# Feed-forward of a hybrid block: up products by seven products of halves, up and down in separate pieces

## The chip, the cores and the metric

The kernel runs on one core of a Trainium2 chip. The metric is the device time of one execution in microseconds: the median of three runs was 3004.93 us before the change (3002.14 to 3009.09). One further execution was profiled, and it gives the trace. The core has four engines for arithmetic that work side by side, each through its own queue in order: TensorE (PE in the rows; PEld is its weight load), VectorE (DVE), ScalarE (ACT) and GpSimd (POOL). SyncE (SP) issues all DMA transfers of this kernel, in order too.

## The reference

One layer over 2048 tokens of 1024 channels: a mixer of three kinds of heads (gated delta rule, mLSTM, S5), an output projection with a residual, and a gated feed-forward with a short causal convolution, again with a residual, and a last norm. The change touches the feed-forward alone:

```
def conv_ffn(x, w_up, conv_w, conv_b, w_down):
    h = causal_depthwise_conv(x @ w_up, conv_w) + conv_b      # 1024 -> 5632, three taps
    gate, up = jnp.split(h, 2, axis=-1)
    return (jax.nn.silu(gate) * up) @ w_down                  # 2816 -> 1024
```

Everything is float32. With 2048 tokens the up product has 2048 x 1024 x 5632 multiplications and the down product half of that.

## The kernel before, in words

A float32 product is made of three faster ones. Each operand is split into a high part (rounded to the format fp32r, by an ACT copy) and a low part (the difference, by a subtraction on POOL or DVE), and `mm` issues for each pair of tiles high x high, high x low and low x high into one PSUM bank.

Work is written as Python generators. `drive` steps them: it keeps a clock of estimated costs, takes the first generator whose needs are met at PE's estimated time, sides before the main one, and lets it emit its next instructions. All engines' calls go through one helper, so that every row of the profile names its line, 167, and the tiles tell the rows apart. The order on each engine is fixed when the program is built. Within one generator the instructions stand in the order of its text, and on the chip each engine takes its queue in that order, waiting at an instruction until what it needs is there.

**Mixer and output projection** (to about 1536 us). `out_proj` runs over 16 tiles of 128 tokens. When the mixer's heads are done, `ffn_pools` opens the pools of the feed-forward, and each tile that is projected is also normed, transposed (`norm2`) and, for the first 1024 tokens, split into the two resident tiles `h2h` and `h2l`; the other 1024 tokens go to memory (`h2_d`). After the last tile `up_first` issues the first four up products.

**Feed-forward** (`ffn`). Tokens come in two halves of 1024, middle channels in 22 tiles of 128; up tile i makes the gate and up tile 22 + i the factor. `jobs` lists, for each half, two up jobs and then a down job over a group of two middle tiles. An up job does, for both sides and both blocks of 512 tokens, one product of 24 matmuls (8 tiles of 128 input channels x 3) into a bank, then the convolution (two small copies of the halo, ACT copy and ACT Identity out of PSUM, two scalar-tensor-tensor on DVE), and for each block Silu, the product and its split into `f_mh` and `f_ml`, which stay in SBUF. A down job does, for 8 tiles of 128 tokens x 2 halves of the output, 6 matmuls into a bank and then adds the bank to `f_acc` in SBUF (DVE), where x plus the output projection already is. Weights are loaded and split (ACT, POOL) by `Weights`, 1024 columns at a time, some tiles ahead. After the last group of a half `final_sums` and `finals` do the last norm and store.

Of the kernel before, what the change touches and what calls it, by code (L numbers as in the profile page):

```python
# [35 lines left out]
Q_BUFS, Z_BUFS = 4, 4  # L36
C_ID, C_TRI, C_CAPT, C_CAPD, C_MASK, C_UP = 0, 1, 2, 3, 4, 5
# [3 lines left out]
def f32(ap):  # L41
    return ap.bitcast(F32)
# [144 lines left out]
class Hybrid:  # L187
# [55 lines left out]
    def params(self):  # L243
# [46 lines left out]
        self.h2_d = self.dram.tile([KD, P, HALF], F32, name="h2_d")  # L290
# [1171 lines left out]
    def part(self, kind):  # L1462
        return self.fw.tile([P, KD, P], F32R, tag=kind, bufs=4, name=kind)

    def raw(self):
        return self.fw.tile([P, KD, P], F32, tag="f_wr", bufs=2, name="f_wr")

# [3 lines left out]
    def ffn_pools(self):  # L1471

        self.wctx.close()
        self.lctx.close()
        self.pctx.close()
        self.ps = self.pool("ps2", space=PSUM)
        self.bufs = {"big": 5, "sd": 3, "y": 1, "yh": 2, "yl": 2}
        kp = self.pool("kp", ctx=self.rctx)
        self.h2t = [kp.tile([P, KD, HALF], F32R, name=f"h2{e}") for e in "hl"]
        self.h2 = [[t[:, k, :] for k in range(KD)] for t in self.h2t]  # L1480
        self.fw = self.pool("fw", ctx=self.rctx)
        self.op = self.pool("op", ctx=self.octx)
        self.ffn_plan()

    def out_proj(self):
# [60 lines left out]
        for i in range(n):  # L1546
# [4 lines left out]
            if i >= n - 2:  # L1551
                self.fws.load()
            if i == n - 1:
                self.fws.split()
# [4 lines left out]
        yield lambda: all(i in self.normed for i in range(HALF // P))  # L1559
        yield from self.up_first()  # L1560

    def norm2(self, i, x, r):

        self.A.activation(out=x, in_=x, func=AF.Copy, scale=r)
        t0 = i * P % HALF
        for j in range(0, KD, 4):
# [15 lines left out]
    class Weights:  # L1582

        def __init__(self, k, order):
            self.k, self.order, self.n = k, order, 0
            self.rawq, self.rdy = [], []

        def load(self):
            if self.n >= len(self.order) or len(self.rawq) >= 2:
                return  # L1590
            kind, m = self.order[self.n]
            self.n += 1
            t, k = self.k.raw(), self.k
            if kind == "u":
                k.S.dma_start(out=t, in_=k.ins["w_up"][0][:, m * P:(m + 1) * P].rearrange("(k p) c -> p k c", p=P))
            else:
                k.S.dma_start(out=t.rearrange("p k c -> p (k c)"), in_=k.ins["w_down"][0][m * P:(m + 1) * P, :])
            self.rawq.append(t)

        def split(self):  # L1600
            if not self.rawq:
                return
            w = self.rawq.pop(0)
            hi, lo = self.k.part("f_wh"), self.k.part("f_wl")
            self.k.split(hi, lo, w)
            self.rdy.append((hi, lo))
            self.load()

        def ahead(self, n):
            if len(self.rdy) < n:  # L1610
                self.split()

        def take(self, n):
            while len(self.rdy) < n:
                self.split()
            r, self.rdy = self.rdy[:n], self.rdy[n:]
            return r

    def ffn_plan(self):
        self.groups = [[m, m + 1] for m in range(0, MF, 2)]  # L1620
        NH = L // HALF

        self.jobs = jobs = []
        for hf in range(NH):
            for gi, g in enumerate(self.groups):
                for j, m in enumerate(g):
                    jobs.append(("U", hf, m))
                    if j == (gi == len(self.groups) - 1) and gi:
                        jobs.append(("D", hf, gi - 1))
            jobs.append(("D", hf, len(self.groups) - 1))  # L1630
        order = []
        for kind, hf, i in jobs:
            order += [("u", i), ("u", MF + i)] if kind == "U" else [("d", m) for m in self.groups[i]]
        self.fws = self.Weights(self, order)

    def up_prod(self, wh, wl, q):
        hh, hl = self.h2
        yield wl, "big"
        ps = self.ps.tile([P, BT], F32, tag="big", bufs=5, name="psf")
        qq = slice(q * BT, (q + 1) * BT)  # L1640
        yield from self.mm3(ps, [(wh[:, k, :], wl[:, k, :], hh[k][:, qq], hl[k][:, qq]) for k in range(KD)])
        return ps

    def up_first(self):
        self.u0 = []
        for side in range(2):
            (wh, wl), = self.fws.take(1)
            for q in range(2):
                self.u0.append((yield from self.up_prod(wh, wl, q)))
                self.fws.ahead(2)  # L1650

    def ffn(self, fp):
        V, A, G, T, S, ins = self.V, self.A, self.G, self.T, self.S, self.ins
# [292 lines left out]
```

## Time and profile before

| | us |
|---|---|
| median of 3 runs | 3004.93 |
| the profiled execution | 3009.54 |
| its span, first to last instruction | 3007.8 |
| PE busy | 2791.7 (93%) |
| DVE busy | 1945.4 (65%) |
| ACT busy | 1165.5 (39%) |
| POOL busy | 821.1 (27%) |
| first up product starts at | 1536.15 |
| last down matmul starts at | 2987.16 |
| mean granted PE clock | 0.965 |

A row of grouped instructions reads: line, engine, operation, output<-inputs by the names of tiles, partitions x elements and types, x count | busy us in all, mean ns of one | idle us of the engine just before them, and who ended it. A row of the timeline reads: start us, length us, engine, line, operation, with the idle time before it in brackets. Matmuls are pipelined, so that a matmul's own duration (389 ns) is longer than the distance to the next one.

### The profile page before, as it was taken

How to read it: one execution, taken by the hardware profiler on the slowest of the kernel's cores; microseconds unless marked ns; L12 is line 12 of the kernel's file. 1: busy time of each engine (PE TensorE's matmuls, PEld its weight loads, DVE VectorE, ACT ScalarE, POOL GpSimd, SP SyncE). 2: the span in 40 equal slices, each digit the busy share in tenths (PEclk: the TensorE clock that was granted, in tenths of full speed). 3: DMA queues.
4: the chain of work that ended last, by engine and by line, in shares of the span. 5: the costliest groups of instructions: out<-in, count | busy, mean ns of one | idle time of the engine just before them, and what ended most of it. 6: DMA issues, size and time to landing. Idle time of an engine off the chain costs nothing.

```text
span 3007.8 us, 37696 instructions
## 1 busy us (share of the span) xinstructions
PE 2791.7 (93%) x13826; PEld 2327.6 (77%) x13826; DVE 1945.4 (65%) x4400; ACT 1165.5 (39%) x2202; POOL 821.1 (27%) x536
## 2 busy tenths in 40 slices
PE   7797789988998989889999999999999999999997
PEld 5686677877886878578888888888888888888885
DVE  6875667678765886664455656566567655656566
ACT  4444344444544354633333332233344323333333
POOL 3261122223322243123222222222222222222223
PEclk9898889989999999989999999999999999999998
DMA  4233212233222324334561111111134111111111
GB/s 121 63 96 94 76 47 77 56 84 103 62 58 68 85 78 123 99 94 141 167 204 42 49 49 50 42 50 56 43 101 165 49 43 49 51 48 50 50 44 62
DMA packets 314944, 232.39 MB, mean 77 GB/s; under 512 B 36291, under 2 KB 286278, under 8 KB 314758
## 3 DMA queue, kind: packets, MB, share of 16 engines
q1 hardware_dynamic: 314758, 229.98, 26.0%
q8 instruction: 109, 1.79, 0.3%
q14 instruction: 77, 0.63, 0.1%
HBM read 192.06 MB, written 37.88 MB: 76 GB/s over the span
## 4 chain that ended last, share of the span: by engine, by line
PE 56%; DVE 3%; ACT 1%; issue 0%; DMA 0%; ACTq 0%; POOL 0%; SPq 0%; DVEq 0%; POOLq 0%
PE psf L167 32%; PE psd L167 16%; PE pso L167 5%; PE psx L167 0%; DVE acc L167 0%; PE sd_pw L167 0%; DVE f_rs L167 0%; PE pz L167 0%; PE sd_p L167 0%; PE sq L167 0%; DVE f_acc L167 0%; ACT junk L167 0%; DVE e_y L167 0%; DVE e_yo L167 0%; PE psq L167 0%
## 5 line engine op out<-in xcount | busy, mean ns | idle before, releaser
L167 POOL TENSOR_TENSOR f_wl<-f_wr,f_wh 128x1024 fp32r<-128x1024 f32 x132 | 341.9, 2591 | 1074.1 <-ACT f_wh L167 1057.1
L167 PE MATMUL psf<-h2h,f_wh 128*128 128x512 f32 x1408 | 547.9, 389 | 0.0
L167 PE MATMUL psf<-h2h,f_wl 128*128 128x512 f32 x1408 | 547.9, 389 | 0.0
L167 PE MATMUL psf<-h2l,f_wh 128*128 128x512 f32 x1408 | 547.7, 389 | 0.0
L167 POOL TENSOR_TENSOR wl<-wr,wh 128x1024 fp32r<-128x1024 f32 x108 | 258.8, 2399 | 589.3 <-ACT wh L167 535.8
L167 DVE SCALAR_TENSOR_TENSOR f_cv<-f_raw,fpar,f_cv 128x512 f32<-128x512 f32 x352 | 266.5, 757 | 76.7 <-ACT f_cv L167 70.3
L167 ACT ACTIVATE f_raw<-psf 128x512 f32<-128x512 f32 x176 | 105.2, 598 | 539.0 <-issue 299.7
L167 PEld LDWEIGHTS psf<-h2h,f_wl 128*128 128x128 f32 x1408 | 264.3, 188 | 54.9
L167 PEld LDWEIGHTS psf<-h2h,f_wh 128*128 128x128 f32 x1408 | 264.3, 188 | 54.9
L167 PEld LDWEIGHTS psf<-h2l,f_wh 128*128 128x128 f32 x1408 | 264.3, 188 | 54.8
L167 DVE TENSOR_TENSOR f_acc<-f_acc,psd 128x512 f32<-128x512 f32 x352 | 229.2, 684 | 116.7 <-PE psd L167 114.1
L167 PE MATMUL psd<-f_wh,f_mh 128*128 128x512 f32 x704 | 278.1, 395 | 0.0
L167 PE MATMUL psd<-f_wl,f_mh 128*128 128x512 f32 x704 | 278.1, 395 | 0.0
L167 PE MATMUL psd<-f_wh,f_ml 128*128 128x512 f32 x704 | 277.9, 395 | 0.0
L167 DVE COPY f_halo<-f_raw 128x2 f32<-128x2 f32 x176 | 73.3, 417 | 278.6 <-ACT f_raw L167 277.5
L167 ACT ACTIVATE f_wh<-f_wr 128x1024 fp32r<-128x1024 f32 x132 | 139.2, 1055 | 269.9 <-issue 263.7
L167 DVE COPY f_raw<-f_halo 128x2 f32<-128x2 f32 x176 | 201.7, 1146 | 0.0
L167 PEld LDWEIGHTS psd<-f_wl,f_mh 128*128 128x128 f32 x704 | 131.9, 187 | 32.4
L167 PEld LDWEIGHTS psd<-f_wh,f_ml 128*128 128x128 f32 x704 | 131.9, 187 | 32.3
L167 PEld LDWEIGHTS psd<-f_wh,f_mh 128*128 128x128 f32 x704 | 131.9, 187 | 32.2
L167 ACT ACTIVATE f_cv<-psf,fpar 128x512 f32<-128x512 f32 x176 | 136.1, 773 | 0.0
L167 ACT ACTIVATE wh<-wr 128x1024 fp32r<-128x1024 f32 x108 | 114.0, 1056 | 38.4 <-PE psz L167 21.1
(496 smaller groups left out, 5574.3 us busy)
## 6 DMA issues: line engine op xcount, KB each, us to landing
wr<-in_w_in_dram SPq DMA_DIRECT2D x104, 512.0 KB
f_wr<-in_w_up_dram SPq DMA_DIRECT2D x88, 512.0 KB
f_wr<-in_w_down_dram SPq DMA_DIRECT2D x44, 512.0 KB
xt<-in_x_dram SPq DMA_DIRECT2D x16, 512.0 KB
y<-y_d SPq DMA_DIRECT2D x16, 512.0 KB
f_acc<-x_d SPq DMA_DIRECT2D x16, 512.0 KB
o_x<-in_x_dram SPq DMA_DIRECT2D x12, 512.0 KB
x_d<-o_x SPq DMA_DIRECT2D x12, 512.0 KB
```

Source lines behind the costliest of these rows:

```text
L167: return f(*args, **kw)
```

## The change: what it does

**Up products.** The 1024 input channels are cut into two halves K1 and K2, the 1024 tokens into two blocks of 512, and gate and up weights of a pair (i, 22 + i) are taken together as a 2 x 2 matrix of halves. Instead of the eight products of halves, seven products of sums and differences of them are made (the scheme with seven products and fifteen sums), and the four results come out of additions. Each product is 4 x 3 = 12 matmuls into one bank. The token side's seven operands (b11, b12, b21, b22 and three sums) are made once for each half by `build`, out of `h2_d`, to which `norm2` now writes all tokens. The weight side's are made per pair by `make`: seven splits of 128 x 512 (ACT, POOL) and four sums on POOL. They go into a ring of 8 (`NPART`), and `make` is called once after each product. The additions of the results are on DVE, each with one operand in PSUM. The halo copies are on ACT now, and Identity reads the sum in SBUF.

**Separate pieces.** For each half, all 22 pairs of up products come first, and then, for each of two blocks of 512 tokens, all of the down product. Middle tiles are stored to memory (`mid_d`) and loaded back; the down weights are read for each block, four times in all instead of twice.

**Down sums.** One block's down product keeps all 8 banks (4 tiles of 128 tokens x 2 halves of the output) and accumulates all 22 x 3 matmuls in each; x2 is loaded and added at the end, and a side `final` does the norm and the store.

**Starts and turns.** `up_first` is gone: `out_proj` waits until the first half's operands are built, all sides finish, then `ffn` opens its pools and makes the first seven parts. Two of the seven operands of the first half are filled by the side `rest_build` during the first pair.

The core of the diff:

```diff
+NRAW, NPART = 4, 8
@@ out_proj
-        yield lambda: all(i in self.normed for i in range(HALF // P))
-        yield from self.up_first()
+        yield lambda: self.built
@@ norm2
-            if i < HALF // P:
-                hi, lo = [t[:, j:j + 4, t0:t0 + P] for t in self.h2t]
-                self.split(hi, lo, h)
-            else:
-                self.S.dma_start(out=self.h2_d[j:j + 4, :, t0:t0 + P].rearrange("k p t -> p k t"), in_=h)
+            self.S.dma_start(out=self.h2_d[j:j + 4, :, i * P:(i + 1) * P].rearrange("k p t -> p k t"), in_=h)
@@ new
+    def rest_build(self, tile):
+        for n in range(2):
+            for j in range(4):
+                x = self.h_part(tile(), 0, j, 1, n)
+                yield x
+                self.put(5 + n, j, x)
+        self.rest = True
+    def split_part(self, w):
+        hi, lo = [self.fq.tile([P, 4, P], F32R, tag="f_" + nm, bufs=NPART, name="f_" + nm) for nm in ("ph", "pl")]
+        self.split(hi, lo, w)
+        self.parts.append((hi, lo))
+        self.ring -= 1
+    def make(self):
+        if not self.todo or self.ring < (1 if self.todo[0][0] == "U" else 2):
+            return
...
+        if kind != "U":
+            w = self.raws.pop(0)
+            for c in range(2):
+                self.split_part(w[:, 4 * c:4 * c + 4, :])
+            self.raw_load()
+            return
...
+        if j == 0:
+            self.split_part(a11)
+        elif j == 1:
+            G.tensor_tensor(out=self.s1, in0=a21, in1=a22, op=ALU.add)
+            G.tensor_tensor(out=self.s2, in0=self.s1, in1=a11, op=ALU.subtract)
+            self.split_part(self.s2)
+        elif j == 2:
+            self.split_part(self.s1)
+        elif j == 3:
+            G.tensor_tensor(out=a21, in0=a11, in1=a21, op=ALU.subtract)
+            self.split_part(a21)
+        elif j == 4:
+            self.split_part(a22)
+        elif j == 5:
+            self.split_part(a12)
+        else:
+            G.tensor_tensor(out=self.s2, in0=a12, in1=self.s2, op=ALU.subtract)
+            self.split_part(self.s2)
...
+    def up_pair(self, hf, i):
...
+        def conv(rw, ci):
+            halo = self.halo2[:, ci, :]
+            cv = tile("cv", 5)
+            A.activation(out=cv, in_=rw[:, 2:BT + 2], func=AF.Identity,
+                         scale=self.fpar[:, 2, ci:ci + 1], bias=self.fpar[:, 3, ci:ci + 1])
+            A.activation(out=rw[:, 0:2], in_=halo, func=AF.Copy)
+            A.activation(out=halo, in_=rw[:, BT:BT + 2], func=AF.Copy)
+            for j in range(2):
+                V.scalar_tensor_tensor(out=cv, in0=rw[:, j:j + BT], scalar=self.fpar[:, j, ci:ci + 1],
+                                       in1=cv, op0=ALU.mult, op1=ALU.add)
+            return cv
+        def mid(ga, up, n):
+            A.activation(out=ga, in_=ga, func=AF.Silu)
+            V.tensor_tensor(out=ga, in0=ga, in1=up, op=ALU.mult)
+            t0 = hf * HALF + n * BT
+            S.dma_start(out=self.mid_d[i, :, t0:t0 + BT], in_=ga)
+        def raw(ps, b):
+            rw = tile("rw", 4, BT + 2)
+            add(rw[:, 2:BT + 2], ps, b)
+            return rw
+        g, u = i, MF + i
+        ps = yield from prod(0)
+        s1 = tile("s1", 2)
+        A.activation(out=s1, in_=ps, func=AF.Copy)
+        self.make()
+        ps = yield from prod(1)
+        u2 = tile("u2", 1)
+        add(u2, ps, s1)
+        self.make()
+        ps = yield from prod(2)
+        w5 = tile("w5", 1)
+        add(w5, ps, u2)
+        self.make()
+        ps = yield from prod(3)
+        u3 = tile("u3", 1)
+        add(u3, ps, u2)
+        r22 = raw(ps, w5)
+        self.make()
+        ps = yield from prod(4)
+        yield lambda: self.rest
+        r21 = raw(ps, u3)
+        up1 = conv(r21, u)
+        up2 = conv(r22, u)
+        self.make()
+        ps = yield from prod(5)
+        ga1 = conv(raw(ps, s1), g)
+        mid(ga1, up1, 0)
+        self.make()
+        ps = yield from prod(6)
+        ga2 = conv(raw(ps, w5), g)
+        mid(ga2, up2, 1)
+        self.make()
@@ down, for each block of 512 tokens
+        groups = [[0], [1]] + [[m, m + 1] for m in range(2, MF, 2)]
+        for gi, ms in enumerate(groups):
...
+            for t in range(NT):
+                for c in range(2):
...
+                    for m, parts in zip(ms, w):
+                        hi, lo = mids[m]
+                        wh, wl = [x.rearrange("p k c -> p (k c)") for x in parts[c]]
+                        self.mm(ps[t, c], (hi[:, tt], lo[:, tt], wh, wl), m == 0, m == MF - 1)
+                    if gi == len(groups) - 1:
+                        a = acc[t, c]
+                        V.tensor_tensor(out=a, in0=a, in1=ps[t, c], op=ALU.add)
+                        A.activation(out=ps[t, c], in_=a, func=AF.Square, accum_out=ss[:, t, c:c + 1])
+                        if c:
+                            self.add_side(final(t))
+                    elif c and nxt:
+                        split(nxt.pop(0))
+                    self.make()
+            self.ring += 2 * len(ms) + (gi < 2)
```

More of the change, by code (lines that the diff above doesn't have):

```diff
@@ L1460, in out_prod @@
         return xs.pop(0)
[L1462 to L1466, printed above, removed]
     def mixed(self):
@@ L1477, in ffn_pools @@
         self.bufs = {"big": 5, "sd": 3, "y": 1, "yh": 2, "yl": 2}
[L1478 to L1480 removed]
+        self.bq = self.operands(self.pool("kp", ctx=self.rctx), 5)
         self.fw = self.pool("fw", ctx=self.rctx)
@@ L1636, in up_prod @@
[L1636 to L1650, printed above, removed]
@@ new lines, in norm2, with operands, put @@
+            self.S.dma_start(out=self.h2_d[j:j + 4, :, i * P:(i + 1) * P].rearrange("k p t -> p k t"), in_=h)
+        self.normed.add(i)
+    def operands(self, pool, n):
+        return [[pool.tile([P, 4, BT], F32R, name=f"b{e}{o}") for e in "hl"] for o in range(n)]
+    def put(self, o, j, x, cols=slice(0, BT)):
+        hi, lo = [t[:, j, cols] for t in self.bq[o]]
+        self.A.activation(out=hi, in_=x, func=AF.Copy)
+        self.V.tensor_tensor(out=lo, in0=x, in1=f32(hi), op=ALU.subtract)
@@ new lines, in ffn @@
+    def ffn(self):
+        S = self.S
+        self.fq = self.pool("fq", ctx=self.rctx)
+        self.bq += self.operands(self.fq, 2)
+        self.fnw = self.fq.tile([P, DM], F32, name="fnw")
+        S.dma_start(out=self.fnw, in_=self.ins["final_norm_w"].unsqueeze(0).to_broadcast([P, DM]))
+        self.halo2 = self.fq.tile([P, 44, 2], F32, name="f_halo")
+        self.V.memset(self.halo2, 0.0)
+        NH, NQ = L // HALF, HALF // BT
+        for hf in range(NH):
+            with ExitStack() as c:
+                self.fu = self.pool("fu", side="right", ctx=c)
+                while len(self.parts) < NPART - 1:
+                    self.make()
+                if hf == 0:
+                    self.rest = False
+                    self.add_side(self.rest_build(lambda: self.fu.tile([P, BT], F32, tag="f_cv", bufs=5, name="f_cv")))
+                else:
+                    yield lambda: self.built
+                for i in range(MF):
+                    yield from self.up_pair(hf, i)
+                self.fu = None
+            with ExitStack() as c:
+                dn = self.pool("dn", side="right", ctx=c)
+                if hf + 1 < NH:
+                    self.built = False
+                    self.add_side(self.build(hf + 1, lambda: dn.tile([P, BT], F32, tag="d_a", bufs=8, name="d_b"), BT))
+                for q in range(NQ):
+                    yield from self.down(hf * NQ + q, dn)
+                yield lambda: not any(sd.gen.__name__ == "final" for sd in self.misc)
```

320 lines of the change are left out of this document (135 added, 185 removed).

## The prediction

> **What bounds the kernel now.** I read the busy shares first, then the 100 us stretches, then the chain of waits of the feed-forward, then single instructions.
>
> ```profile
> span 3007.8 us, 37696 instructions
> 1400.00:1536.00 136.00, 133.82 (x646) 111.23 (x645) 57.43 (x194) 53.03 (x87) 46.52 (x27) 1.00 0.55 167
> 1602.00:2976.00 1374.00, 1374.00 (x6003) 1125.75 (x6002) 854.02 (x1223) 446.72 (x674) 330.42 (x128) 1.00 0.19 56
> 1624.99 43.53 PE psf L167 x192
> 1668.52 22.39 PE psd L167 x96
> L167 PE MATMUL psf<-h2h,f_wh 128*128 128x512 f32 x1408 | 547.9, 389 | 0.0
> L167 PE MATMUL psd<-f_wh,f_mh 128*128 128x512 f32 x704 | 278.1, 395 | 0.0
> 2987.16 0.39 PE L167 MATMUL psd<-f_wh,f_ml 128*128 128x512 f32 x1
> ```
>
> The two stretches read: length, then busy us of PE, PEld, DVE, ACT and POOL, granted clock, DMA share, GB/s. In the feed-forward PE is busy 1374 of 1374 us at full clock, and nothing else is near it. From the chain, an up matmul takes 43.53 / 192 = 0.2267 us and a down matmul 22.39 / 96 = 0.2332 us. There are 3 x 1408 = 4224 up and 3 x 704 = 2112 down matmuls: 957.6 + 492.5 = 1450.1 us, which is the whole way from 1536 to the last matmul at 2987.6. So matmuls taken out here come off one for one, as long as PE stays the slowest.
>
> **What seven products save.** A pair of channel tiles over 1024 tokens costs 2 x 2 x 8 x 3 = 96 matmuls before, 21.8 us. Afterwards it is 7 products x 4 x 3 = 84, 19.0 us. The slower psd rate says that a bank change costs about 0.05 us (6 matmuls a bank take 1.399, 24 take 5.441), so I take 19.4 us a pair. Over 44 pairs that is 104 us less PE work. The down matmuls stay 2112.
>
> **What the seven products ask of the other engines.** These rows give the prices.
>
> ```profile
> L167 DVE SCALAR_TENSOR_TENSOR f_cv<-f_raw,fpar,f_cv 128x512 f32<-128x512 f32 x352 | 266.5, 757 | 76.7 <-ACT f_cv L167 70.3
> L167 ACT ACTIVATE f_cv<-psf,fpar 128x512 f32<-128x512 f32 x176 | 136.1, 773 | 0.0
> 1697.75 1.54 DVE L167 SCALAR_TENSOR_TENSOR f_cv<-f_raw,fpar,f_cv 128x512 f32<-128x512 f32 x2 [0.50 <-ACT f_cv L167]
> L167 DVE TENSOR_TENSOR f_acc<-f_acc,psd 128x512 f32<-128x512 f32 x352 | 229.2, 684 | 116.7 <-PE psd L167 114.1
> L167 DVE TENSOR_TENSOR f_cv<-f_cv 128x512 f32<-128x512 f32 x78 | 53.4, 685 | 0.0
> L167 ACT ACTIVATE f_cv<-f_cv 128x512 f32<-128x512 f32 x78 | 48.7, 624 | 0.0
> L167 ACT ACTIVATE h2h<-n_h x16: 630/632/635, 1400.9 to 1450.6; 128x512 fp32r<-128x512 f32 x16
> L167 POOL TENSOR_TENSOR h2l<-n_h,h2h x16: 1285/1298/1303, 1401.6 to 1452.7; 128x512 fp32r<-128x512 f32 x16
> L167 DVE COPY f_raw<-f_halo 128x2 f32<-128x2 f32 x176 | 201.7, 1146 | 0.0
> L167 ACT ACTIVATE halo<-psk 128x3 f32<-128x3 f32 x12 | 2.0, 169 | 0.0
> ```
>
> Per pair POOL now does seven splits and four sums of weights (S1, S2, a21, and S2 rewritten), all 128x512: 11 x 1.30 = 14.3 us. DVE does seven additions out of PSUM (0.68), eight scalar-tensor-tensor (0.76) and two products (0.69): 12.2 us. ACT does a copy, seven splits, four Identities, eight two-column copies and two Silus: about 11 us. Each alone fits under 19.4. The halo copies leave DVE, where those into f_raw took 1.15 us on the mean; that was off the path.
>
> But the queues are in order, and `make` stands between the products in the text of `up_pair`: ACT's high part of S2, of a21 and of the last sum waits for POOL, and the convolutions of the next product wait behind it on ACT. I follow this once around, from the convolution after product 4 to the same place a pair later, each step released by the one before:
>
> - ACT Identity and one halo copy 0.94; DVE four scalar-tensor-tensor (two convolutions) 3.08; DVE add of product 5 0.68; ACT 0.94; DVE 1.54; ACT Silu 0.62; DVE product 0.69;
> - DVE add of product 6 0.68; ACT 0.94; DVE 1.54; ACT Silu 0.62; ACT high part of part 6 0.63;
> - POOL, in its own order, the low parts of part 6 and of part 0 of the next pair, S1, S2: 5.20; ACT high part of S2 0.63; POOL low parts 1 and 2, a21: 3.90; ACT high part of a21 0.63, and behind it on ACT the Identity with which this began.
>
> That is **23.3 us a pair against PE's 19.4**. Handovers (0.08 us from ACT to POOL, 1697.60 + 1.06 to 1698.74 in the next fence) are paid for by durations that overlap a little on one engine. The seven parts made ahead shift PE against this loop, but don't shorten it: PE has to wait for low parts.
>
> **The port.** POOL and DVE get in each other's way:
>
> ```profile
> 2226.74 2.40 POOL L167 TENSOR_TENSOR f_wl<-f_wr,f_wh 128x1024 fp32r<-128x1024 f32 x1 [14.80 <-ACT f_wh L167]
> 2227.14 3.08 DVE L167 TENSOR_TENSOR h2l<-f_hx,h2h 128x1024 fp32r<-128x1024 f32 x1
> 2224.80 1.23 DVE L167 TENSOR_TENSOR h2l<-f_hx,h2h 128x1024 fp32r<-128x1024 f32 x1 [0.26 <-ACT h2h L167]
> 1741.27 5.10 DVE L167 TENSOR_TENSOR f_acc<-f_acc,psd 128x512 f32<-128x512 f32 x8
> 1741.65 2.41 POOL L167 TENSOR_TENSOR f_wl<-f_wr,f_wh 128x1024 fp32r<-128x1024 f32 x1 [12.91 <-ACT f_wh L167]
> 1697.60 1.06 ACT L167 ACTIVATE f_wh<-f_wr 128x1024 fp32r<-128x1024 f32 x1
> 1698.74 2.80 POOL L167 TENSOR_TENSOR f_wl<-f_wr,f_wh 128x1024 fp32r<-128x1024 f32 x1 [4.92 <-ACT f_wh L167]
> ```
>
> A DVE subtraction of two SBUF tiles takes 1.23 us alone and 3.08 beside a POOL one: it ends 1.1 us after POOL does. Eight additions with a PSUM operand run at full pace beside POOL, and a POOL operation that starts during a scalar-tensor-tensor takes 2.80 instead of 2.40. So the eight scalar-tensor-tensor and the two products of a pair exclude POOL's eleven operations, in both directions. Four POOL operations (low parts 3, 4, 5 and the last sum, 5.2 us) fall into the loop's DVE stretch. The toll is between 0 and 5.2 us; the row at 2227.14 lost 1.85 of a possible 2.40. I take half, 2.6, because some of the four fall on additions from PSUM or on ACT's steps. **So 25.9 us a pair, 1139.6 us in all.**
>
> **The rest of the sum**, along the span.
>
> ```profile
> 1536.15 0.48 PE L167 MATMUL psf<-h2h,f_wh 128*128 128x512 f32 x1
> 1539.73 2.39 POOL L167 TENSOR_TENSOR f_wl<-f_wr,f_wh 128x1024 fp32r<-128x1024 f32 x1 [14.91 <-ACT f_wh L167]
> 1539.88 2.25 DVE L167 SCALAR_TENSOR_TENSOR n_rs<-ss,n_rs 128x1 f32<-128x1 f32 x1
> 1543.38 1.15 ACT L167 ACTIVATE o_x<-o_x,n_rs 128x1024 f32<-128x1024 f32 x1 [3.73 <-DVE n_rs L167]
> 1514.02 0.39 SPq L167 DMA_DIRECT2D y<-y_d  x1
> 1518.88 1.06 ACT L167 ACTIVATE yh<-y 128x1024 fp32r<-128x1024 f32 x1 [0.55 <-DMA y<-y_d]
> 2998.61 0.57 DVE L167 TENSOR_SCALAR f_rs<-f_rs 128x2 f32<-128x2 f32 x3
> 3000.78 0.16 DVE L167 SCALAR_TENSOR_TENSOR f_rs<-f_ss,f_rs 128x2 f32<-128x2 f32 x1
> 3001.04 1.33 ACT L167 ACTIVATE f_acc<-f_acc,f_rs 128x512 f32<-128x512 f32 x2 [5.26 <-DVE f_rs L167]
> ```
>
> - Up to 1536.1 nothing changes. The sums of halves (72 DVE operations of 256 columns, an estimated 0.35 us each from the 0.68 for 512: 25 us) begin when tile 7 is normed, about 1454, and DVE is idle 58% of the stretch 1400 to 1536. If that cover were gone, they would be late by up to those 25 us.
> - The first up products filled the time in which tile 15 is normed; now all sides finish first. Without the POOL split that held DVE for 2.1 us, ACT's scaling ends at 1542.4, then the first split: **+6.3**.
> - The eight late loads of `rest_build` stand on SP behind two weight loads, which wait for POOL's last sum; ACT and DVE take 8 x (0.63 + 0.69) for them. Between 0 and 14 us; I take **+7**.
> - Per half: the first pair makes its own seven parts before its convolutions (11 x 1.30 and some splits, about 17), the last one makes none (the 11 of the POOL steps go away): +6. Then the last middle tile is stored, the first ones are loaded (the 512 KB load above took 4.9 from issue to use; I estimate 3 for 256 KB) and split, 7.3 in all, before the third group. Twenty middle tiles x 24 x 0.2332 = 111.9. The second block is 123.1 + 1.2 for more bank changes. Between the blocks DVE owes eight additions (5.4) and three finals of 4.0 (13 small operations at 0.195, as in the rows from 2998.61, and two of 0.76) from the first full bank at 1.4: 18.9 against PE's 11.2. It is 7.7 late on the last bank, which is asked for again after 4.9, with a square of 0.6 between: 3.4. Sum **253** a half.
> - Between the halves PE stands until that last addition, its square and the first split: **+9**.
> - Tail: 7.7, square 0.8, small operations 2.5, two products 1.5, and from ACT's last end at 3002.4 to the end of the span 5.4: **18**, where it is 20.2 now.
> - The 352 additions to f_acc in SBUF are gone (229 us of DVE), and this costs or wins nothing: PE was not waiting for them. The middle tiles' way through memory and the second reading of the down weights are 768 KB per 5.6 us, 140 GB/s; the stretch 1400 to 1536 moved 167 at a DMA share of 0.55. SP holds them in order, but each load is asked for two groups ahead.
>
> 1536.1 + 6.3 + 7 + 1139.6 + 506 + 9 + 18 = **3222 us** of span; 1.7 lie around it in the profiled execution (3009.5), which itself was 4.6 above the median of the runs (3004.9). I say **3220 us**, 7% slower.
>
> **Rivals.** All have the same fixed 2082 us; only the pair differs. Break-even with 3007.8 is 21.0 us a pair.
>
> 1. The loop without a toll: 23.3, **3108 us**. For it: in 88 products f_cv<-f_cv DVE was never delayed. Against: POOL was idle there; now it is busy more than half the time.
> 2. The port alone: ACT's waits fall under it, and POOL's 14.3 and DVE's 7.4 just alternate: 21.7, **3037 us**. [...]
> 3. Not slower: the parts made ahead take up the waits, and PE sets the pace with 19.4: **2936 us**. It decides if the pair is under 21.0. For it: PE is full now and no engine is asked for more than 14.3 us. Against: the loop above, in which PE has no part.
> 4. The clock. PE would idle some 6 us in each pair.
>
> ```profile
> 300.00:400.00 100.00, 78.61 (x415) 68.34 (x414) 61.40 (x219) 38.02 (x92) 16.35 (x12) 0.82 0.22 62
> 1254.00:1262.00 8.00, 3.61 (x5) 1.62 (x6) 6.84 (x26) 3.61 (x6) 0.00 (x0) 0.51 0.00 0
> 1294.00:1302.00 8.00, 7.07 (x37) 6.51 (x37) 3.89 (x16) 3.76 (x7) 0.66 (x1) 0.66 0.02 5
> ```
>
> At the 0.82 of a stage that is 79% busy, 19.4 become 23.7, still under 25.9: no change. At the 0.66 of the short stretch, 29.4: **3376 us**. [...]
>
> **Chances and range.** The forecast 0.64, the loop without toll 0.16, the port alone 0.08, PE alone 0.05, the clock 0.06, a pair within 0.2% of break-even 0.01. A toll between 1.6 and 5.2 gives 3178 to 3336 for the forecast; the next two cases reach down to 3037. Range 3030 to 3340. A difference under 0.2% can't be told from none here. Faster 0.05, same 0.01, slower 0.94.
>
> **What will show it.** In the up stretches PE busy near 75%, waiting for the low parts that POOL writes; ACT waiting for POOL's sums; the mean of the scalar-tensor-tensor above 0.85 us; one pair every 26 us in the chain. In the down stretches PE near 100%. The prediction is wrong if PE is full in the up stretches, or if a pair comes under 23 us, or if more than 60 us go to the starts and the turns between up and down.

## The result

The changed kernel takes **3214.24 us** (median of 4 runs, 3213.01 to 3215.72), where the kernel before took 3003.61 in the same session: 1.0698 times as long, with a 95% interval of 1.0679 to 1.0716. The prediction had said 3220. The profiled execution has a span of 3213.3 us.

From the page of the changed kernel: the span and two groups of the feed-forward (busy us, mean ns of one, then idle time ahead and what ended it).

```profile
span 3213.3 us, 39006 instructions
L169 POOL TENSOR_TENSOR f_pl<-f_wr,f_ph 128x512 fp32r<-128x512 f32 x360 | 520.6, 1462 | 576.3 <-ACT f_ph L169 576.3
L169 DVE SCALAR_TENSOR_TENSOR f_cv<-f_rw,fpar,f_cv 128x512 f32<-128x512 f32 x352 | 344.3, 989 | 399.7 <-ACT f_rw L169 393.4
```

The scalar-tensor-tensor, 757 ns on the mean before, takes 989; POOL's subtraction takes 1462 ns where 1.30 us had been put for it. No engine is full any more: PE, busy 93% of the span before, is busy 87% of it. How fast the pairs go by is read from the queue of SP, which stores two middle tiles at the end of each pair:

```profile
2020.68 5.46 SPq L169 DMA_DIRECT2D mid_d<-f_cv  x2
2045.58 5.45 SPq L169 DMA_DIRECT2D mid_d<-f_cv  x2
```

**24.9 us a pair.** The forecast was 25.9; break-even was 21.0. And these are ACT's waits over the whole span (us in total, times, longest):

```profile
ACT f_ph L169 <- POOL f_S L169: 204.9, 46, 14.1
ACT f_ph L169 <- POOL f_wr L169: 149.8, 44, 4.7
```

44 pairs, and ACT waits about once in each of them for POOL's S2 and once for its a21, 4.5 and 3.4 us on the mean: the two places at which the prediction had let the loop pass from POOL to ACT. Part of one pair in order of time (start, length, engine, operation, and in brackets the idle time ahead with its releaser), without PE and SP, and with other rows left out at the dots:

```profile
1704.40 1.28 POOL L169 TENSOR_TENSOR f_S<-f_wr 128x512 f32<-128x512 f32 x1
...
1705.76 1.28 POOL L169 TENSOR_TENSOR f_S<-f_S,f_wr 128x512 f32<-128x512 f32 x1
1707.07 1.15 ACT L169 ACTIVATE f_ph<-f_S 128x512 fp32r<-128x512 f32 x2 [4.22 <-POOL f_S L169]
1707.78 2.54 POOL L169 TENSOR_TENSOR f_pl<-f_S,f_ph 128x512 fp32r<-128x512 f32 x2 [0.74 <-ACT f_ph L169]
1710.28 1.28 POOL L169 TENSOR_TENSOR f_wr<-f_wr 128x512 f32<-128x512 f32 x1
1711.59 0.63 ACT L169 ACTIVATE f_ph<-f_wr 128x512 fp32r<-128x512 f32 x1 [3.37 <-POOL f_wr L169]
1712.13 0.80 ACT L169 ACTIVATE f_cv<-f_rw,fpar 128x512 f32<-128x512 f32 x1
1712.30 1.29 POOL L169 TENSOR_TENSOR f_pl<-f_wr,f_ph 128x512 fp32r<-128x512 f32 x1 [0.74 <-ACT f_ph L169]
...
1713.06 4.23 DVE L169 SCALAR_TENSOR_TENSOR f_cv<-f_rw,fpar,f_cv 128x512 f32<-128x512 f32 x4 [7.41 <-ACT f_rw L169]
...
1722.91 1.29 POOL L169 TENSOR_TENSOR f_S<-f_wr,f_S 128x512 f32<-128x512 f32 x1
1723.38 2.16 DVE L169 SCALAR_TENSOR_TENSOR f_cv<-f_rw,fpar,f_cv 128x512 f32<-128x512 f32 x2 [0.98 <-ACT f_rw L169]
```

Read it from the top: POOL makes S1 and S2 (1704.40, 1705.76), ACT has stood for 4.22 us and splits S2, POOL makes two low parts and then a21 (1710.28), ACT has stood for 3.37 us and splits a21, and only then comes the Identity of the convolution that has been in its queue all along (1712.13); DVE has been idle for 7.41 us. Its four scalar-tensor-tensor then take 4.23 instead of 3.08, since POOL is in its next low part when they start. Later in the pair two more take 2.16 us instead of 1.54, beside POOL's last sum (1722.91).

### The profile page after: what moved, and what is told of

It is laid out like the page before. It is cut to its first block, busy times and chain, and to the rows that moved or that the text cites. A ratio compares the mean times of both kernels' runs of the same rounds, so it can differ in the third digit from the quotient of the medians.

```text
span 3213.3 us, 39006 instructions
## 1 busy us (share of the span) xinstructions
PE 2804.3 (87%) x13298; PEld 2261.1 (70%) x13298; DVE 1862.8 (58%) x4296; ACT 1305.6 (41%) x2818; POOL 1342.9 (42%) x1046
## 5 line engine op out<-in xcount | busy, mean ns | idle before, releaser
L169 POOL TENSOR_TENSOR f_pl<-f_wr,f_ph 128x512 fp32r<-128x512 f32 x360 | 520.6, 1462 | 576.3 <-ACT f_ph L169 576.3
L169 PE MATMUL psf<-bh,f_ph 128*128 128x512 f32 x1232 | 515.9, 419 | 93.6 <-ACT f_ph L169 85.3
L169 DVE SCALAR_TENSOR_TENSOR f_cv<-f_rw,fpar,f_cv 128x512 f32<-128x512 f32 x352 | 344.3, 989 | 399.7 <-ACT f_rw L169 393.4
L169 PE MATMUL psf<-bh,f_pl 128*128 128x512 f32 x1232 | 520.1, 422 | 50.0 <-POOL f_pl L169 49.3
L169 PE MATMUL psf<-bl,f_ph 128*128 128x512 f32 x1232 | 507.0, 411 | 0.6 <-DVE bl L169 0.6
L169 PEld LDWEIGHTS psf<-bh,f_ph 128*128 128x128 f32 x1232 | 244.3, 198 | 177.3 <-ACT f_ph L169 116.7
L169 PEld LDWEIGHTS psf<-bl,f_ph 128*128 128x128 f32 x1232 | 244.5, 198 | 58.1 <-DVE bl L169 1.1
L169 PE MATMUL psd<-f_ph,d_l 128*128 128x512 f32 x640 | 253.4, 396 | 18.2 <-DVE d_l L169 18.1
L169 PE MATMUL psd<-f_ph,d_h 128*128 128x512 f32 x640 | 252.5, 395 | 4.8 <-ACT d_h L169 4.8
L169 PE MATMUL psd<-f_pl,d_h 128*128 128x512 f32 x640 | 252.1, 394 | 0.1
```

Source lines behind the costliest of these rows:

```text
L169: return f(*args, **kw)
```

## The experiments

In this section "changed" is the changed kernel (24.9 us a pair, 3214). Each edit is made on it, unless another is named. A time stands beside its ratio to the kernel before on the same chip, or alone where there was one run.

### Is it the loop? POOL's sums earlier (e1_sums_early)

```diff
-            self.s1, self.s2 = [self.fu.tile(... for nm in ("S1", "S2")]
-            G.tensor_tensor(out=self.s1, in0=a21, in1=a22, op=ALU.add)
-            G.tensor_tensor(out=self.s2, in0=self.s1, in1=a11, op=ALU.subtract)
+            self.s1, self.s2 = self.nexts
             self.split_part(self.s2)
...
         elif j == 3:
-            G.tensor_tensor(out=a21, in0=a11, in1=a21, op=ALU.subtract)
             self.split_part(a21)
...
         elif j == 5:
             self.split_part(a12)
+            self.G.tensor_tensor(out=self.s2, in0=a12, in1=self.s2, op=ALU.subtract)
...
+                self.sums(pieces(self.raws[2:4]))   (S1, S2 and a21 of the next pair)
```

> The changed kernel, with POOL's three weight sums of the next pair (S1, S2, a21) and the last sum of this pair moved in POOL's queue to right behind low part 5, where POOL idles; ACT's high parts then find them done. Same instructions, same counts. The changed kernel takes 24.9 us a pair (from one pair's stores to the next) and 2118 us besides. Theory (the loop through ACT waiting for POOL's sums sets the pair): the loop loses POOL's sums, and the next limit decides: 21.7 us if POOL and DVE exclude each other on the port, 2118 + 44 x 21.7 = 3073 us; 19.4 if only PE is left, 2971 us. Rival (the port as a whole, or PE at a lowered clock, sets 24.9 already): no change, 3214 us.

3074.37 us, ratio 1.0227 (1.0212 to 1.0242). From SP's queue, and then DVE's group on the page:

```profile
1705.67 6.70 SPq L169 DMA_DIRECT2D mid_d<-f_cv  x2
1727.06 6.71 SPq L169 DMA_DIRECT2D mid_d<-f_cv  x2
```

```profile
L169 DVE SCALAR_TENSOR_TENSOR f_cv<-f_rw,fpar,f_cv 128x512 f32<-128x512 f32 x352 | 464.9, 1330 | 135.4 <-ACT f_rw L169 129.1
```

21.4 us a pair: the same work in another order takes 3.5 us less a pair, and the kernel is 140 us shorter. So the loop was the bound. (44 times 3.5 would be 154 us. The last pair of each half prepares no next one and takes 20.1 to 20.2 us in both kernels; the 42 intervals between the stores of the two halves take 1036.5 us in the changed kernel and 897.1 here, which is the 140.) DVE waits 129 us for ACT where it had waited 393. What is left is near the port's figure of 21.7 and not PE's 19.4, and the scalar-tensor-tensor now take 1330 ns on the mean, with POOL busy 339 of the 450 us from 1600 to 2050.

### Is there a port? The taps' second operand from PSUM (e2_taps_psum)

```diff
-                V.scalar_tensor_tensor(out=cv, in0=rw[:, j:j + BT], scalar=..., in1=cv, ...)
+                V.scalar_tensor_tensor(out=cv, in0=ps, scalar=..., in1=rw[:, j:j + BT], ...)
...
-        mid(ga1, up1, 0)
+        mid(ga1, ps, 0)
```

> The changed kernel, with the second operand of the convolution's scalar-tensor-tensor and of the middle product taken from the product's PSUM bank, so that DVE has only one SBUF input in each; order and counts as in the changed kernel. Its convolution and its middle are not those of the reference. Theory (a loop of 23.3 us, and 1.6 us of toll on the port): 23.3 us a pair, 3143 us. Rival 1 (the port alone sets the pair): the pair falls to PE's 19.4, 2971 us. Rival 2 (no toll): 3214 us.

3136.46 us, ratio 1.0431 (1.0410 to 1.0451). SP's stores, then the same six taps of a pair as above, and the groups of DVE and POOL within 1600 to 2000:

```profile
1713.62 4.84 SPq L169 DMA_DIRECT2D mid_d<-f_cv  x2
1736.68 4.84 SPq L169 DMA_DIRECT2D mid_d<-f_cv  x2
```

```profile
1729.16 2.98 DVE L169 SCALAR_TENSOR_TENSOR f_cv<-psf,fpar,f_rw 128x512 f32<-128x512 f32 x4 [7.47 <-ACT f_rw L169]
1738.23 1.54 DVE L169 SCALAR_TENSOR_TENSOR f_cv<-psf,fpar,f_rw 128x512 f32<-128x512 f32 x2 [0.98 <-ACT f_rw L169]
L169 DVE SCALAR_TENSOR_TENSOR f_cv<-psf,fpar,f_rw 128x512 f32<-128x512 f32 x138 | 102.1, 750 | 163.4 <-ACT f_rw L169 161.0
L169 POOL TENSOR_TENSOR f_pl<-f_wr,f_ph 128x512 fp32r<-128x512 f32 x69 | 89.2, 1292 | 106.6 <-ACT f_ph L169 106.6
```

With one operand in PSUM the same DVE instruction takes 750 ns and POOL's 1292, beside each other; with both operands in SBUF the two groups take 985 and 1428 ns over the same 400 us of the changed kernel, and 1360 and 1517 in e1_sums_early. That delay is all that "the port" stands for here: what makes it was not shown. 23.06 us a pair is the loop without a toll, for which the prediction had 23.3. So the toll in the changed kernel is 24.9 - 23.06 = **1.8 us a pair**, where 2.6 had been taken. It can be seen in place: the four taps take 2.98 instead of 4.23, the last two 1.54 instead of 2.16, together 1.87 us less. The edit also frees the taps from the Identity's result; that did not shorten the loop, since DVE still waits for ACT's halo copy (f_rw) ahead of them, 7.47 us here and 7.41 in the changed kernel.

### Is PE in it? Half of the up matmuls (e3_half_pe)

```diff
-            yield from self.mm3(ps, [(hi[:, k, :], ...) for k in range(4)])
+            yield from self.mm3(ps, [(hi[:, k, :], ...) for k in range(2)])
```

> The changed kernel, with half of the matmuls of each up product left out (2 of 4 pieces of the contraction), everything else as it is. Theory (PE is not in the loop): the pair stays at 24.9 us, the whole within 15 us of 3214. Rival (PE, slowed by its clock after gaps, sets the pair): the pair falls with PE's work, by 3 us or more, 3080 us or less.

3221.32 us. The stretch 1600 to 2050 (length, busy us of PE, PEld, DVE, ACT, POOL, granted clock, DMA share, GB/s), and the stores:

```profile
1600.00:2050.00 450.00, 288.12 (x770) 166.53 (x768) 245.63 (x309) 178.97 (x399) 261.07 (x199) 0.78 0.21 63
```

```profile
1705.98 5.45 SPq L169 DMA_DIRECT2D mid_d<-f_cv  x2
1730.79 5.44 SPq L169 DMA_DIRECT2D mid_d<-f_cv  x2
```

With half of the products' matmuls gone a pair takes 24.8 us as before, and the granted clock goes to 0.78 without anything coming later. PE and its clock have no part in the pace. This also excludes the rival of the clock.

### The sums left out (e4_no_sums), and both edits at once (e5_early_taps)

```diff
-        if j == 0: ...   (S1, S2, a21, the last sum, each split)
+        self.split_part((a11, a21, a22, a21, a22, a12, a12)[j])
```

> The changed kernel, with POOL's four weight sums of each pair left out (the plain pieces are split instead, so the results are not those of the reference); PE, ACT and DVE have the same instructions as before. Theory: ACT no longer waits for sums, the port has 7 x 1.30 + 7.4 = 16.5 us, and PE sets the pair with 19.4 us: 2971 us, which also checks the 2118 us besides the pairs. Rival (DVE's and ACT's own chain of convolutions is the limit): above 22 us a pair, over 3086 us.

> Both earlier edits at once: POOL's sums early, and DVE's taps and middle product with one operand in PSUM (so its convolution and middle are not the reference's). The kernel with early sums alone took 21.4 us a pair. Theory (those 21.4 are the port that POOL and DVE share): without the port PE sets the pair, 19.7 us as in the kernel without sums: 2114 + 44 x 19.7 = 2981 us. Rival (they are the chain of ACT and DVE, or POOL's own 14.3 us with its waits): the pair stays near 21.4, 3056 us or more.

2981.81 and 2999.47 us. The stretch 1600 to 2050 and the stores of e4_no_sums; e5_early_taps joins the edits of e1_sums_early and e2_taps_psum:

```profile
1600.00:2050.00 450.00, 441.32 (x1874) 353.79 (x1873) 303.58 (x392) 224.96 (x499) 213.75 (x160) 0.99 0.32 100
```

```profile
1706.80 4.85 SPq L169 DMA_DIRECT2D mid_d<-f_cv  x2
1726.48 4.85 SPq L169 DMA_DIRECT2D mid_d<-f_cv  x2
```

The stores of both settle at **19.68 us a pair** (in e5_early_taps at 1714.32 and 1734.00, for example), with PE busy 98% of the stretch at a clock of 0.99. This is PE's own pace, 84 matmuls 0.2343 us apart without a wait, for which 19.4 had been taken. With the taps' operand out of SBUF the 21.4 of e1_sums_early falls to it too, so those 21.4 were the port. The layers come off one by one: loop 24.9, port 21.4, PE 19.7. e4_no_sums is 11 us above its expected 2971 because the pair is 19.68 and not 19.4: 44 x 19.68 = 866, so 2980.0 - 866 = 2114 us are fixed part, near the changed kernel's 3213.3 - 44 x 24.9 = 2118. e5_early_taps is 18 us above its 2981, outside the pairs: by the same count its fixed part is 2132. Some 10 of these 14 us more than in the changed kernel are a matter of counting, since the last pair of each half is 4.8 us shorter than the others there and not here. The prediction had 2082. The later runs ask where the 36 us between 2082 and 2118 are.

### A repaired order (e6_sums_dve)

The sums go to DVE, a pair ahead and behind the additions of product 3, and DVE makes the additions of products 5 and 6 ahead of the taps of the convolution before.

```diff
-            G.tensor_tensor(out=self.s1, ...)          # at part 1
+            self.V.tensor_tensor(out=s1, ...)          # in sums(), at part 3 of the pair before
...
+        r11 = raw(ps, s1)
+        ga1 = conv_a(r11, g)
+        conv_v(r22, u, up2)
         self.make()
         ps = yield from prod(6)
+        r12 = raw(ps, w5)
+        ga2 = conv_a(r12, g)
+        conv_v(r11, g, ga1)
```

> The reference's computation in full. The four weight sums go to DVE (0.61 us each there, 1.28 on POOL), one pair ahead, behind the additions of product 3; and DVE's additions of products 5 and 6 stand ahead of the taps of the product before, so that ACT's Identity and Silu are covered. The port then has 7 x 1.28 + 8 x 0.73 + 6 x 0.61 = 18.5 us, under PE's 19.7. Theory: PE sets the pair, 19.7 us, 2118 + 867 = 2985 us, below the kernel before by 0.7%. Rival (18.5 of 19.7 us on a port with first come, first served still makes loops through ACT late): 20.5 to 21.4 us a pair, 3020 to 3060 us.

3007.56 us, ratio 1.0004 (0.9992 to 1.0016): no different from the kernel before, and between the two times expected. Two of its stores:

```profile
1702.19 1.13 SPq L169 DMA_DIRECT2D mid_d<-f_cv  x2
1722.83 1.13 SPq L169 DMA_DIRECT2D mid_d<-f_cv  x2
```

These two are 20.6 us apart; over the whole run the intervals go from 19.9 to 21.5 and are **20.27 us** on the mean, without the last two of each half (16.9 and 15.5). With the prediction's fixed part the pairs had 3007.8 - 2082 = 926 us to stay under, and they take 44 x 20.27 = 892: 34 us would have been won. But the fixed part of this kernel, its span of 3010.5 less 892, is 2119, as in the changed kernel and not 2082, and that takes them back.

### Where the fixed part grew: the out-projection (e8_late_loads, e9_build_late, e10_build_steps)

The out-projection's products, first and last start, in the kernel before and in the changed one:

```profile
L167 PE MATMUL pso<-woh,yh x256: 387/389/774, 1305.2 to 1534.7; 128*128 128x512 f32 x128
```

```profile
L169 PE MATMUL pso<-woh,yh x256: 387/389/774, 1296.0 to 1547.6; 128*128 128x512 f32 x128
```

229.5 us have become 251.6, in a stretch in which the prediction had let nothing change. One trace each doesn't give this to a microsecond: the same row in the eight other runs that leave the stretch as it is (e1 to e6, e11 and e12) gives 247.1 to 254.9. Three causes were tried. First, the four weight loads now stand at the start of the stretch; in e8_late_loads they come when three token tiles are left:

```diff
-        for _ in range(NRAW):
-            self.raw_load()          # in ffn_plan
+            if i == n - 3:           # in out_proj
+                for _ in range(NRAW):
+                    self.raw_load()
```

> The changed kernel with the one edit that the four weight tiles are loaded three token tiles before the end of the output projection. In the changed kernel the last projection product ends 11 us later than before the change, and PE idled between 1376 and 1400 us for x and y tiles that were loaded beside 2 MB of weights. Theory (the weight loads delay the x and y tiles): about 5 us of the 11 come back. Rival (the tiles for the sums of halves, written and read back, or DVE, delay it): the last projection product ends where it did, within 2 us.

3229.23 us; the out-projection took 254.0 us, inside that spread. The loads aren't it. Second, the building of the seven operands, which shares the stretch:

```diff
-        self.add_side(self.first_build())          # in ffn_pools
+        self.add_side(self.first_build())          # in out_proj, behind its loop
         yield lambda: self.built
```

> The changed kernel with one edit: the building of the first half's operands begins only when the last product of the out-projection is in the queues, so that its 32 loads, 96 splits and sums no longer stand between the out-projection's own steps. The out-projection, from its first product to its last, took 229.5 us in the kernel before and 251.6 in the changed one. Theory (the build holds ACT and SP ahead of the splits of y): the length comes down to 230 to 240. Rival (the stores of the normed half to memory, which also are new in this stretch, and the traffic: PE already lost 4.6 of the 22 us between 1350 and 1450, before the build begins): it stays above 245. Either way the build now stands alone behind the last normed tile, some 25 to 40 us before the first high part, so that the whole time goes up, to about 3225 to 3240 by the theory and 3240 to 3255 by the rival.

3230.99 us, and the same row reads

```profile
L169 PE MATMUL pso<-woh,yh x256: 387/389/774, 1294.4 to 1533.0; 128*128 128x512 f32 x128
```

238.6 us, 8.5 under the shortest of the others: **some 13 of the 22 us (8 to 16 by the spread) belong to the build**. They come back at the end of the out-projection, only to be spent behind it, where the build now stands alone. The other 9 or so stay. The stretch 1350 to 1400 lies long before any build. In it PE is busy 44.90 of 50 us in e9_build_late, where it was 48.85 in the kernel before, and the DMA share is 0.62 where it was 0.46: the first half's normed tiles now go to memory as well, 256 KB at a time. That these stores are the 9 us is argued from the two windows, which lie 11 us apart in the course of the out-projection, and not shown by a run.

Third, whether the build's waits or its work do it. In e10_build_steps, made on e6_sums_dve, its splits are only put in ACT's queue when the sum should be there, and its loads in SP's when their tiles should be free:

```diff
                 for o, x in ((3, b22), (2, b12), (1, b11), (4, b21)):
+                    yield x
                     self.put(o, j, x, cols)
+                yield self.bq[4][1]
```

> The kernel with the sums on DVE (e6_sums_dve, 3007.6 us, out-projection 253.8 us) with one edit: in the build the splits of each sum are only put in ACT's queue when the sum is expected to be ready, and the next four loads only in SP's queue when the tiles that they fill are expected to be free. Theory (waits of the build hold the queues of ACT and SP): about half of the 24 us comes back, 2992 to 2998, faster than the kernel before. Rival (the work and the transfers themselves are late, not the waits): 3003 to 3010, no change.

3011.67 us, ratio 1.0018 (1.0008 to 1.0027). The out-projection took 248.2 us, where e6_sums_dve has 254.9; both lie inside the spread, so a gain isn't shown. The last split of the build began at 1558.5 instead of 1522.6, behind the out-projection's last product. The expectation of 2992 to 2998 was wrong, and its rival, no change, held: the build has to be done somewhere, and this order found no free cover for it. How much of the growth is waits in the queues and how much is the work itself stays open.

### Where the fixed part grew: the turns (e7_turns, e11_turn_pool, e12_turn_memory)

The first products behind the changed kernel's first half, whose last down matmul ends at 2375.19, with other rows left out at the dots:

```profile
2377.24 0.50 PE L169 MATMUL psf<-bh,f_ph 128*128 128x512 f32 x1 [2.05 <-ACT f_ph L169]
...
2391.29 1.15 ACT L169 ACTIVATE f_ph<-f_S 128x512 fp32r<-128x512 f32 x2 [14.10 <-POOL f_S L169]
2391.97 0.80 PE L169 MATMUL psf<-bh,f_ph 128*128 128x512 f32 x1 [9.24 <-ACT f_ph L169]
```

PE goes on after 2 us, not after the 9 of the prediction, makes one product, and then stands 9.24 us more for POOL's S2, which is late. In e6_sums_dve the sums stand on DVE behind the four norms of the last block, and PE waits 12.7. In e7_turns I changed three things of e6_sums_dve at once: the weight loads of e8_late_loads, the first half's late operands asked for ahead of the first parts, and the norm's small tiles in a pool that lives as long as the feed-forward.

```diff
-        ss = dn.tile([P, NT, 2], F32, tag="d_ss", bufs=2, name="d_ss")
+        ss = self.fq.tile([P, NT, 2], F32, tag="d_ss", bufs=2, name="d_ss")
```

> The kernel with the sums on DVE and three edits at the starts and turns: the four weight tiles of the feed-forward are loaded three token tiles before the end of the output projection instead of at its beginning; the late operands' loads are issued ahead of the weight loads that wait for POOL, and the last norm's weight after them; the small tiles of the last norm lie in another pool, so that POOL's first sums after the turn don't wait for the norm. Theory: 5 + 7 + 10 us off what is besides the pairs: 22 us less than with the sums on DVE alone, 2963 us if that takes 2985. Rival (these stalls lie beside others): less than 8 us.

3022.26 us, ratio 1.0054 (1.0035 to 1.0073): 15 us slower than e6_sums_dve, not 22 faster. Two more runs took it apart. e11_turn_pool is e6_sums_dve with the first pair's sums on POOL, which stands idle at the turn (15.38 us in e6_sums_dve, up to 2296.67); e12_turn_memory is that with the small tiles moved as above.

```diff
             if self.nexts is None:
-                self.sums(pieces(self.raws[0:2]))
+                self.sums(pieces(self.raws[0:2]), self.G)
```

> The kernel with the sums on DVE (e6_sums_dve, 3007.6 us) with one edit: the three sums ahead of the first pair of a half go to POOL. In e6_sums_dve they stand on DVE behind the last norms of the half before, from 2285 to 2294.4, and PE waits 12.70 us for them. But the memory in which POOL would write is that of the last norm's small tiles, as in the changed kernel, where POOL waited 10.2 us for DVE there. Theory (the memory holds the sums, whatever engine makes them): PE still waits 9 to 13 us at the turn, 3004 to 3009 us. Rival (the queue of DVE holds them): the wait falls under 4 us, 2995 to 2999.

> e11_turn_pool with one more edit: the small tiles of the norm stand in memory of their own, as they did in e7_turns. Theory: now nothing that POOL writes is held by DVE, and PE waits under 4 us at the turn, 2995 to 2999, faster than the kernel before. Rival: e7_turns lost 9 us in the down products, each of which took 393 ns in the middle instead of 389, and if that comes from where the small tiles (and so all the tiles behind them) lie in memory, it comes back here, 3003 to 3010.

3009.47 us (ratio 1.0012, 0.9997 to 1.0026) and 3020.33 (1.0048, 1.0030 to 1.0066): the first as its theory had it, the second above both of its numbers. The longest wait at the turn is 9.3 us in the first and 9.4 in the second. So DVE's queue was 3 of the 12.7, and the memory of the small tiles nothing: in e12_turn_memory POOL still waits as it did,

```profile
POOL f_S L169 <- DVE d_ss L169: 10.2, 1, 10.2
```

though d_ss lies elsewhere now. My reading of that row in the changed kernel, that S2 is written where d_ss lay, falls. What of DVE's norms POOL waits for stays open.

The 11 us between the two kernels are in the down products, whose records differ (min, median and max ns; first and last start), in e11_turn_pool and in e12_turn_memory:

```profile
L169 PE MATMUL psd<-f_ph,d_h x640: 387/389/796, 2018.0 to 2977.0; 128*128 128x512 f32 x160
```

```profile
L169 PE MATMUL psd<-f_ph,d_h x640: 387/393/793, 2029.1 to 2999.4; 128*128 128x512 f32 x160
```

From the third group to the last product the two halves' down stretches take 246.5 and 240.9 us in the first, 251.1 and 246.5 in the second (the traced execution of e11_turn_pool, 2998.47 us, is the shortest of its ten; the rest of its lead lies elsewhere). That is 10.2 us more, for an edit that only changes where small tiles (32 and 8 bytes a partition), and so the tiles behind them, lie in memory. e7_turns has the median of 393 too, and 9.1 us more than e6_sums_dve in the same stretches. That explains 9 of its 15; the other 6 stay open.

## Why the prediction was right

The sum was 3222 of span against 3213.3. Step by step:

| step | predicted, us | measured, us | difference |
|---|---|---|---|
| 44 pairs | 44 x 25.9 | 44 x 24.9 | -44 |
| start: first split of an up weight | 1542.4 | 1553.7 | +11.3 |
| first half: from there to the third down group, less 22 pairs | 20.3 | 26.7 | +6.4 |
| first half: down, third group to the end | 239.6 | 247.0 | +7.4 |
| between the halves | 9 | 16.8 | +7.8 |
| second half: to the third down group, less 22 pairs | 13.3 | 14.7 | +1.4 |
| second half: down, third group to the end | 239.6 | 240.0 | +0.4 |
| tail | 18 | 18.8 | +0.8 |

The measured points are the first and last starts in these rows of the changed kernel, with the turn's rows above:

```profile
L169 ACT ACTIVATE f_ph<-f_wr x24: 613/618/633, 1553.7 to 1696.1; 128x512 fp32r<-128x512 f32 x24
...
L169 PE MATMUL psd<-f_ph,d_h x320: 388/389/792, 2128.2 to 2374.3; 128*128 128x512 f32 x160
...
L169 PE MATMUL psd<-f_ph,d_h x320: 387/389/628, 2954.5 to 3193.7; 128*128 128x512 f32 x160
```

- **The loop was right, and shown to be the bound.** 23.3 without a toll against the 23.06 of e2_taps_psum; earlier sums took 140 us off; less PE work took nothing. The three rivals for the pair were right too as layers: the port's 21.7 came as 21.4, a little under the sum of the two engines' operations, and PE's 19.4 as 19.7. None of them decided, because the loop lay on top.
- **PE's 19.4 came near by two errors.** The prediction read the slower down matmuls of the kernel before as a bank change of 0.05 us. In that trace every down matmul, inside a bank too, follows the one before by 0.233 us (1668.36, 1668.59, 1668.82, 1669.05, 1669.29 in its timeline), so there is no such term. And the up matmuls of the changed kernel go at 0.2343 us, not at the 0.2267 of the kernel before.
- **The toll was mis-sized**: 2.6 taken, 1.8 measured as the difference to e2_taps_psum. I had taken half of 5.2 for want of a row. In the pair shown, POOL's low part that begins at 1712.30 is more than half done when DVE's four taps begin at 1713.06, and these are 1.25 us longer than in e2_taps_psum; the last sum stretches the last two taps by 0.62. The fourth operation, low part 5 at 1721.67, runs beside an addition out of PSUM, which takes its usual 0.68.
- **"Up to 1536.1 nothing changes" was wrong.** The prediction looked for cover for the build on DVE, which has it, and not on ACT and SP, in whose queues the build's splits and loads stand between the out-projection's own. The build is some 13 us of the 22 that the out-projection grew (e9_build_late); that it acts through these two queues is argued, and e10_build_steps didn't bear it out. The out-projection began 9 us earlier in this execution, so that only 13 of the 22 show in the table, as +11.3 with a start that was 1.7 shorter than the 6.3 given to it.
- **The turn between the halves was wrong**: 9 predicted, 16.8 measured. The prediction let PE stand until the first split and forgot that the second product needs S2, which is behind the norms.
- **The first half's way to its third down group was put 6.4 us too short.** It is 12.0 longer than the second half's, where the late operands had been given 7 of a possible 14. No run took them out alone.
- **Down came out near by two errors.** The down matmuls were taken at 0.2332 us from the kernel before; in the changed kernel eight banks follow each other every 1.36 us, six matmuls at 0.2267 (DVE's additions at 2234.94, 2236.30 and 2237.66 show it), 6.6 us less for the 1008 of a half. But at the change of blocks PE waits 6.2 us for a low part behind DVE's norms, where 3.4 had been put, and stands again:

```profile
2248.00:2272.00 24.00, 16.48 (x59) 0.79 0.47 158
```

  PE is busy 16.5 of these 24 us (length, PE's busy us, clock, DMA share, GB/s). The first half has some 4 us of waits for DVE's low parts besides, between 2142 and 2180. The second half has the same wait of 6.2 us and hardly another, and comes to 240.0 by chance.
- **The announced signs**: the scalar-tensor-tensor above 0.85 us (0.989), ACT waiting for POOL's sums, a pair near 26 us (24.9), PE near 100% in down but for the change of blocks: as said. PE near 75% in the up stretches was not what the profile shows:

```profile
1600.00:2100.00 500.00, 439.97 (x1708) 328.10 (x1706) 272.15 (x343) 197.74 (x442) 290.26 (x220) 0.96 0.22 64
```

  That is 88%, though 84 matmuls at 0.2343 are 19.7 us of the pair's 24.9, 79%. The rest is in how the records are spaced. Of the 70 matmuls of these 500 us that start behind a wait of over 0.1 us, 62 are recorded as 0.50 or 0.51 us instead of 0.39 or 0.40 (as also at 2377.24 above). And the mean clock of 0.96 is not an even one: for stretches of 3.4 us it is 0.50, and 8 matmuls start where 16 do just after:

```profile
1703.20:1706.60 3.40, 3.34 (x8) 2.67 (x9) 2.44 (x4) 0.00 (x0) 3.32 (x4) 0.50 0.88 225
1706.80:1710.20 3.40, 3.40 (x16) 2.76 (x15) 0.00 (x0) 1.15 (x2) 2.66 (x3) 1.00 0.37 110
```

  So the sign was badly chosen, and the step behind it, PE waiting in each pair, was right. That the clock halves in this way costs the pairs nothing: it does so twelve times between 1600 and 2100, and all the intervals between the stores there are 24.87 to 24.95 us. With e3_half_pe, 24.8 us a pair at a mean of 0.78, this excludes the rival of the clock.
- **One sign of being wrong did come.** The prediction named more than 60 us for the starts and the turns. By the table the start (1553.7 - 1536.1 = 17.6), the two ways to the third down group (26.7 and 14.7) and the turn (16.8) are 75.8 us, where 48.9 had been put. So by its own sign this part of the sum was wrong.

The total is nearer than its parts, by luck: the pair was put 1.0 us too high, 0.8 of it the toll, which is 44 us too much; the starts, the turns and down were put 36 us too low.

## What to carry to other kernels

Before counting what a change saves on the busiest engine, follow the queues once around the new inner loop, each step released by the one before: a sum made by one engine and split by another, with the consumer's next work queued behind the split, made 24.9 us a pair where no engine was asked for more than 19.7. When this loop was broken, the next layer was the operations with which two engines held each other up (21.4, by sum 21.7), and only behind that did the saving on the busiest engine show (19.68). For work that is moved beside other work, look for cover in each queue that it passes, not only on the engine with the most idle time.

## What had not been expected of the hardware

- **Busy PE is not working PE.** 88% busy at a needed 79%. Pace is better read from repeated marks, such as the stores, than from the busy share.
- **The same matmul has two paces.** Down, 6 take 1.40 us in the kernel before (with records of 395 ns) and 1.36 in the changed kernel. Up it is the other way round: 0.2267 us each before, 0.2343 in the changed kernel and in e4_no_sums. In e12_turn_memory moving two small tiles alone brought the median record from 389 to 393 ns and cost 10 us over the two halves. Which property of the place decides wasn't tried.
- **The clock halves without a long gap.** Between 1600 and 2100 no wait of PE in the changed kernel is longer than 1.5 us, and yet the clock falls to 0.50 twelve times, for 3.41 us each. In the 3.41 us ahead of each fall PE's records cover 38 to 50%; in the 122 other such windows at the full clock they cover 53% or more. Whether this share is what decides was not tried by a run.
- **Beside POOL even 128x1 instructions of DVE took 1.20 us instead of 0.16**, in the changed kernel at the turn (DVE's and POOL's rows):

```profile
2377.16 0.16 DVE L169 TENSOR_TENSOR d_ss<-d_rs 128x1 f32<-128x1 f32 x1
2377.36 1.20 DVE L169 SCALAR_TENSOR_TENSOR d_ss<-d_ss,d_rs 128x1 f32<-128x1 f32 x1
2378.59 1.20 DVE L169 SCALAR_TENSOR_TENSOR d_rs<-d_ss,d_rs 128x1 f32<-128x1 f32 x1
```

  The two scalar-tensor-tensor take 1.20 us, where the others in this norm take 0.16, and end with POOL's subtraction of 2377.26 and its sum of 2378.50, of 1.28 and 1.27 us.
